# Attention's query transposes: whole words, two heads at a time, with the split into halves moved behind the transpose

## The chip, the cores and the metric

The kernel runs on one core of one Trainium2 chip. The metric is device time in microseconds (us), the median of several runs; lower is better. A core has TensorE (PE, matrix products and transposes, writing to PSUM), VectorE (DVE), ScalarE (ACT), GpSimd (POOL) and SyncE (SP), which issues the loads. In the profile, PEld is TensorE's loading of weights.

## The reference

One layer of a hybrid decoder block, for one sequence of 512 tokens and width 1024, float32 throughout. The input is normalised and projected once; two token mixers work side by side; their outputs are gated per channel, merged and projected again.

```python
h = rms_norm(x, norm_pre); proj = h @ w_in      # then split by columns
q_n = apply_rotary(q_n.reshape(B, S, 8, 64), nsa_ang)   # k_c, k_s, k_w too
o_a = nsa_sequence(q_n, k_c, v_c, k_s, v_s, k_w, v_w, gate)   # sparse attention
y_a = (o_a * silu(z_n)) @ w_nsa_o
o_b = retention_sequence(q_r, k_r, v_r)
y_b = (o_b * silu(z_r)) @ w_ret_o
x = x + rms_norm((sigmoid(m_a) * y_a + sigmoid(m_b) * y_b) @ w_out, norm_post)
```

The attention has 8 heads of 64 channels in two key groups, and three branches (compressed, selected, sliding window). Each head's scores are `q · k * 64 ** -0.5`, masked, put through softmax, and multiplied with the values. With 512 tokens there are only 8 selectable blocks, so every valid block is selected, and selected and sliding branch both see all earlier tokens.

## The kernel before

**Number format.** TensorE is fed in fp32r, the rounded form of float32. A float32 operand is split into a high half, rounded to fp32r, and a low half, the rest; three products (high-high, low-high, high-low) replace one. A split is a rounding copy (on ScalarE through `act`, or for weights on ScalarE or VectorE through `cp_any`) and a subtraction on VectorE (`sub_split`). The weights come as a stream of 128x1024 pieces into `raw`; `splitter` and `split_lo` turn each into two pieces `whi` and `wlo` of 512 columns, held in rings of nine.

**Order.** Every part is a Python generator, and `Order.run` chooses which goes on next by priority and by running estimates of when each engine is free (`Order.eng`, `Order.now`). What comes out is one fixed order of instructions per engine; at run time the engines wait for each other through semaphores. The choice of engine in `cp_any`, and of the engine for the softmax scaling in `att_head`, also goes by these estimates. Buffers that are passed around are in rings: four `NAT` tiles, two PSUM banks each for `ACC` (projections), `PS` (scores), `PT` (transposes) and `PO` (attention outputs).

**Stages.** `main` runs the large products in order: the keys and values of two branches, then 280 columns with the third, then the queries (four tiles of 128 tokens, t = 3, 2, 1, 0, all 512 columns of 8 heads), then `hidden` (the compression network, twice, with products of 256 columns), and then the gates, retention and output blocks. As each query tile's product ends, `tail_q(t)` takes it: a scaled copy from PSUM to a `NAT` tile (`qn`), the rotation (`rope16`), the split into halves, transposes, and a copy into `qT[t]`. When `qT[t]` and the keys are ready, `attention` starts `att_cmp` and the `att_head`s of that tile, whose blocks share TensorE with `main`.

**Layout of the queries.** `qT[t]` is 128 partitions by 8 heads by 128 tokens, fp32r. For each head the 64 channels' high half lies on partitions 0 to 63 and the low half on 64 to 127. The keys `kA` (high) and `kB` (low) hold the same 64 channels twice, on both halves of the partitions, so that one product sums over both halves of the query. The compressed keys `kc` are doubled in the same way. Before the transpose, the same memory (`qs`) holds the split halves in token order.

**Names in the profile.** The helpers have one line each: `act` is L189, `V.tensor_copy` in `cp_any` L197, `tt` (and so `sub_split`) L201, `ts` L210, `mm` L222, `tr` L226, the masked row maximum of `att_head` L801. `arena_r` holds all fp32r arrays (`qT`, keys, values), `arena_f` the float32 ones, `nat` the `NAT` tiles, `bank` all of PSUM. `ident` is the float32 identity for transposes and `identr` the same in fp32r; only `tail_q` uses `identr`.

Of the kernel before, what the change touches and what calls it, by code (L numbers as in the profile page):

```python
# [11 lines left out]
FR = mybir.dt.float32r  # L12
# [6 lines left out]
P = 128  # L19
# [12 lines left out]
LAG, PE_LAG = 55.0, 60.0  # L32
# [104 lines left out]
def block_kernel(ctx: ExitStack, tc, x, xT, x0s, ws, small, w2s, norm_post, rope_r, dmask, out):  # L137
# [10 lines left out]
    ep = ctx.enter_context(tc.tile_pool(name="end", bufs=1))  # L148
# [6 lines left out]
    def at(kb, n, dt=FT):  # L155
        o = int(kb * 256)
        return (arena_r if dt == FR else arena_f)[:, o:o + n]

    def f(ap):
        return ap.bitcast(FT)  # L160

    banks = [pp.tile([P, 512], FT, name=f"bank{i}") for i in range(8)]
    ACC, PS, PT, PO = (Ring(b, PE_LAG) for b in (banks[0:2], banks[2:4], banks[4:6], banks[6:8]))
# [15 lines left out]
    def act_ns(o, i, k=0):  # L179
        return 0.833 * size(o) + (51 if far(i) else 93) + 93 * k  # L180
# [4 lines left out]
    def lazy(*vals):  # L185
        return sum(v is not None and not isinstance(v, (int, float)) for v in vals)

    def act(o, i, func=AF.Copy, r=0.0, **kw):
        S.activation(o, i, func, **kw)  # L189
        return od.op("act", act_ns(o, i, lazy(kw.get("bias"), kw.get("scale"))) + (95 if "accum_out" in kw else 0), r)  # L190
# [9 lines left out]
    def tt(o, a, b, op, r=0.0, e="dve"):  # L200
        (V if e == "dve" else G).tensor_tensor(o, a, b, op=op)  # L201
        if op == OP.pow:
            return od.op(e, 300 + 164 * size(o), r, True)
        return od.op(e, (1.042 * size(o) + 69) if e == "dve" else (2.36 * size(o) + 77), r, e == "pool" or near(o, a, b))
# [20 lines left out]
    def tr(ps, a, idn, r=0.0):  # L225
        T.transpose(ps, a, idn)  # L226
        return od.pe(86 if a.dtype == FR else 108, r, 45.0 if a.dtype == FR else 31.0)
# [6 lines left out]
    def sub_split(lo, src, hi, r, e="dve"):  # L234
        return tt(lo, src, f(hi), OP.subtract, r, e)
# [4 lines left out]
    ident = cp.tile([P, P], FT, name="ident")  # L240
    make_identity(nc, ident)
    identr = cp.tile([P, P], FR, name="identr")
# [10 lines left out]
    qT = [at(4 * t, 1024, FR).rearrange("p (h c) -> p h c", h=8) for t in range(NT)]  # L253
# [228 lines left out]
    def rs(t, i=0):  # L482
        return rs3[:, i, t:t + 1]
# [16 lines left out]
    def rope16(v, t, shape, r, e="dve"):  # L500

        n = int(np.prod(shape))
        pat = {1: "p (a c) -> p a c", 2: "p (a b c) -> p a b c"}[len(shape)]
        kw = dict(zip("ab", shape))
        t1, t2 = (at(41 + 0.5 * i, n * 16).rearrange(pat, **kw) for i in range(2))

        def bc(a):
            c = a.shape[-1]
            for _ in shape:
                a = a.unsqueeze(1)  # L510
            return a.broadcast_to([P, *shape, c])
        ix = (slice(None),) * (1 + len(shape))
        lo, hi, al = ix + (slice(0, 8),), ix + (slice(8, 16),), ix + (slice(0, 16),)
        tt(t1, v[al], bc(ropen[:, t, 0:16]), OP.mult, r, e)
        tt(t2[lo], v[hi], bc(ropen[:, t, 16:24]), OP.mult, r, e)
        r = tt(t2[hi], v[lo], bc(ropen[:, t, 24:32]), OP.mult, r, e)
        return tt(v[al], t1, t2, OP.add, r, e)
# [184 lines left out]
    def tail_q(t, ps, e):  # L702
        qn = yield from NAT.get()
        yield e, "act"
        e = act(qn, ps, r=e, scale=rs(t, 1))
        ACC.put(ps, e)
        yield e, "dve"
        e = rope16(qn.rearrange("p (h c) -> p h c", h=8), t, (8,), e)
        qs = qT[t].rearrange("p h (s c) -> p h s c", s=2)
        qv = qn.rearrange("p (h c) -> p h c", h=8)  # L710
        e = act(qs[:, :, 0, :], qv, r=e)
        yield e, "dve"
        e = sub_split(qs[:, :, 1, :], qv, qs[:, :, 0, :], e)
        NAT.put(qn, e)
        for g in range(2):
            pt = yield from PT.get()
            yield e + PE_LAG
            for j in range(4):
                ep = tr(pt.bitcast(FR)[:, j * P:(j + 1) * P],
                        qs[:, g * 4 + j].rearrange("p a b -> p (a b)"), identr, e)  # L720
            yield ep, "act"
            ep = act(qT[t][:, g * 4:g * 4 + 4, :], pt.rearrange("p (h c) -> p h c", h=4), r=ep)
            PT.put(pt, ep)
        qready[t] = ep
        od.flags.add(f"q{t}")

# [468 lines left out]
    def main():  # L1195
# [29 lines left out]
        for t in reversed(range(NT)):  # L1225
            ps, e = yield from nat(blk, t, 512, t == 0)
            od.spawn(tail_q(t, ps, e), 1)
# [161 lines left out]
```

## Time and profile before

| | |
|---|---|
| median of 3 runs | 530.89 us (529.78 to 530.95) |
| span of the profiled execution, first to last instruction | 527.0 us |
| the profiled execution's own whole time | not listed; its span stands 3.9 us under the median |
| TensorE busy | 518.6 us (98%) |
| VectorE busy | 376.9 us (72%) |
| ScalarE busy | 272.8 us (52%) |
| GpSimd busy | 12.6 us (2%) |
| mean granted TensorE clock | 0.999 |

The median of the runs is what is compared between kernels. The span holds what the profile shows; around it lies time that no row covers. Busy shares are means over the whole span and hide that stages have different limits. A matmul's row is longer than the step to the next matmul, because matmuls overlap, so TensorE's rows are best read by their starts. The chain that ended last says which engine's work, or which wait, set the time of each stretch.

### The profile page before, as it was taken

To read this page: it belongs to the slowest core of one execution; us is meant where nothing else is said; L and a number is where in the kernel's file an instruction comes from. 1 tells how busy PE (TensorE), PEld (TensorE's weight loads), DVE (VectorE), ACT (ScalarE), POOL (GpSimd) and SP (SyncE) were. 2 spreads that over 40 slices of the span, in tenths; PEclk is the share of its full clock that TensorE was granted. 3 is DMA by queue.
4 is the path that set the end of the run, shared out by engine and by line. 5 is a ranking of instruction groups with operands and counts; after the bars stand their busy time and mean duration, and the time that the engine had idled before them with its cause. 6 is when DMAs were issued, how large, how long until landed. Compare 5 with 4: busy or idle time off the path is not lost.

```text
span 527.0 us, 7380 instructions
## 1 busy us (share of the span) xinstructions
PE 518.6 (98%) x2634; PEld 437.5 (83%) x2634; DVE 376.9 (72%) x921; ACT 272.8 (52%) x592; POOL 12.6 (2%) x32
## 2 busy tenths in 40 slices
PE   9999999999999999999999999999999999999995
PEld 7888788888888888888888888888888888888885
DVE  6699799889879999887886576777637335345533
ACT  6664698687657888574535253625304324123411
POOL 1000000000000000000000000000000000000000
PEclk9999999999999999999999999999999999999999
DMA  8951027502204004133131341131905134304032
GB/s 320 370 183 41 21 81 214 186 2 90 71 1 137 24 5 156 40 106 114 41 120 44 137 157 44 48 115 40 326 34 159 33 127 138 104 1 159 1 99 100
DMA packets 18133, 55.19 MB, mean 105 GB/s; under 512 B 1969, under 2 KB 3249, under 8 KB 18097
## 3 DMA queue, kind: packets, MB, share of 16 engines
q1 hardware_dynamic: 17952, 54.60, 31.0%
q8 instruction: 20, 0.33, 0.3%
q14 instruction: 17, 0.13, 0.1%
q10 hardware_dynamic: 144, 0.14, 0.1%
HBM read 52.63 MB, written 2.10 MB: 104 GB/s over the span
## 4 chain that ended last, share of the span: by engine, by line
PE 89%; DVE 4%; DMA 4%; issue 2%; ACT 1%; SPq 0%; POOLq 0%; DVEq 0%; POOL 0%
PE bank L222 82%; PE bank L226 6%; DMA raw<-in_stream_dram 4%; DVE wlo L201 1%; DVE arena_r L201 0%; DVE arena_f L801 0%; ACT arena_f L189 0%; DVE arena_f L210 0%; DVE whi L197 0%; DVE arena_f L201 0%; SPq L435 0%; DVE arena_f L214 0%; SPq L315 0%; DVE stat L218 0%; ACT whi L189 0%
## 5 line engine op out<-in xcount | busy, mean ns | idle before, releaser
L189 ACT ACTIVATE whi<-raw 128x512 fp32r<-128x512 f32 x148 | 88.5, 626 | 50.7 <-PE bank L222 43.6
L201 DVE TENSOR_TENSOR wlo<-raw,whi 128x512 fp32r<-128x512 f32 x160 | 103.6, 684 | 5.7 <-ACT whi L189 4.2
L222 PE MATMUL bank<-whi,hTh 128*128 128x512 f32 x256 | 100.4, 408 | 0.2 <-ACT hTh L189 0.2
L222 PE MATMUL bank<-whi,hTl 128*128 128x512 f32 x256 | 96.5, 392 | 0.0
L222 PE MATMUL bank<-wlo,hTh 128*128 128x512 f32 x256 | 96.1, 391 | 0.0
L222 PE MATMUL bank<-arena_r 128*128 128x256 f32 (+2 forms) x328 | 69.9, 335 | 0.0
L222 PE MATMUL bank<-hTh,whi 128*128 128x512 f32 x160 | 63.8, 399 | 0.0
L222 PE MATMUL bank<-hTh,wlo 128*128 128x512 f32 x160 | 62.5, 390 | 0.0
L222 PE MATMUL bank<-hTl,whi 128*128 128x512 f32 x160 | 62.4, 390 | 0.0
L189 ACT ACTIVATE arena_f<-arena_f,stat 128x512 f32<-128x512 f32 (+3 forms) x106 | 56.8, 560 | 6.2 <-DVE stat L218 2.8
L222 PE MATMUL bank<-arena_r,whi 128*128 128x512 f32 x192 | 59.1, 389 | 0.0
L189 ACT ACTIVATE arena_r<-bank 128x512 fp32r<-128x512 f32 (+2 forms) x80 | 44.6, 569 | 25.8 <-PE bank L226 25.5
L201 DVE TENSOR_TENSOR arena_r<-bank,arena_r 128x512 fp32r<-128x512 f32 (+2 forms) x72 | 46.6, 655 | 15.0 <-ACT arena_r L189 14.5
L222 PEld LDWEIGHTS bank<-whi,hTl 128*128 128x128 f32 x256 | 48.4, 189 | 10.8
L222 PEld LDWEIGHTS bank<-arena_r 128*128 128x128 f32 x328 | 51.6, 189 | 6.9 <-DVE arena_r L201 0.4
L222 PEld LDWEIGHTS bank<-whi,hTh 128*128 128x128 f32 x256 | 48.5, 190 | 8.8 <-ACT hTh L189 0.5
L222 PEld LDWEIGHTS bank<-wlo,hTh 128*128 128x128 f32 x256 | 48.3, 189 | 8.2
L222 PE MATMUL bank<-whi,arena_r 128*128 128x512 f32 (+1 forms) x176 | 49.2, 353 | 0.0
L222 PEld LDWEIGHTS bank<-arena_r,whi 128*128 128x128 f32 x192 | 36.0, 188 | 7.6 <-DVE sg L214 0.2
L226 PE MATMUL bank<-ident,arena_f 128*128 128x128 f32 (+1 forms) x244 | 36.7, 273 | 1.0 <-DVE arena_f L522 1.0
L222 PE MATMUL bank<-arena_r,wlo 128*128 128x512 f32 x96 | 37.4, 389 | 0.0
L222 PEld LDWEIGHTS bank<-whi,arena_r 128*128 128x128 f32 x176 | 32.1, 189 | 4.5
(125 smaller groups left out, 656.2 us busy)
## 6 DMA issues: line engine op xcount, KB each, us to landing
raw<-in_stream_dram SPq DMA_DIRECT2D x79, 512.0 KB, 4.1
arena_f<-in_x_dram SPq DMA_DIRECT2D x8, 512.0 KB, 7.0
arena_f<-in_rope_r_dram SPq DMA_DIRECT2D x8, 256.0 KB, 2.7
arena_f<-in_xT_dram SPq DMA_DIRECT2D x7, 256.0 KB, 5.9
out_dram<-arena_f SPq DMA_DIRECT2D x6, 256.0 KB, 2.1
raw<-in_stream_dram SPq DMA_DIRECT2D x4, 280.0 KB, 7.5
raw<-in_stream_dram SPq DMA_DIRECT2D x2, 256.0 KB, 3.2
arena_f<-in_norm_post_dram SPq DMA_DIRECT2D x1, 512.0 KB, 7.5
```

The source lines that it names most:

```text
L189: S.activation(o, i, func, **kw)
L201: (V if e == "dve" else G).tensor_tensor(o, a, b, op=op)
L222: T.matmul(ps, a, b, start=start, stop=stop)
L226: T.transpose(ps, a, idn)
```

## The change

Before, `tail_q` split the rotated queries in SBUF, transposed the halves as fp32r in two groups of four heads (each transpose takes the 128 columns of one head, high beside low), and copied each group from PSUM into `qT`. Now it transposes the rotated float32 queries, four transposes of 128 columns that each hold two heads. An even head then lies on partitions 0 to 63 of the PSUM bank and an odd head on 64 to 127. ScalarE rounds each half of the partitions into `qT` on the same partitions (the high halves), and VectorE subtracts these from the bank and writes the low halves to the other 64 partitions. So an even head has its high half on partitions 0 to 63, as before, and an odd head has the low half there. The keys are untouched, since they are the same on both halves. The `NAT` tile is given back after the transposes and no longer after the split; one `PT` bank is taken where two were, and it is given back after the last subtraction. Nothing outside `tail_q` differs in the source.

```diff
         e = rope16(qn.rearrange("p (h c) -> p h c", h=8), t, (8,), e)
-        qs = qT[t].rearrange("p h (s c) -> p h s c", s=2)
-        qv = qn.rearrange("p (h c) -> p h c", h=8)
-        e = act(qs[:, :, 0, :], qv, r=e)
-        yield e, "dve"
-        e = sub_split(qs[:, :, 1, :], qv, qs[:, :, 0, :], e)
+        pt = yield from PT.get()
+        yield e + PE_LAG
+        for i in range(4):
+            e = tr(pt[:, i * P:(i + 1) * P], qn[:, i * P:(i + 1) * P], ident, e)
         NAT.put(qn, e)
-        for g in range(2):
-            pt = yield from PT.get()
-            yield e + PE_LAG
-            for j in range(4):
-                ep = tr(pt.bitcast(FR)[:, j * P:(j + 1) * P],
-                        qs[:, g * 4 + j].rearrange("p a b -> p (a b)"), identr, e)
-            yield ep, "act"
-            ep = act(qT[t][:, g * 4:g * 4 + 4, :], pt.rearrange("p (h c) -> p h c", h=4), r=ep)
-            PT.put(pt, ep)
+        qp = qT[t].rearrange("p (i o) c -> p i o c", o=2)
+        pv = pt.rearrange("p (i c) -> p i c", i=4)
+        rows = (slice(0, 64), slice(64, P))
+        yield e, "act"
+        for o in range(2):
+            eh = act(qp[rows[o], :, o, :], pv[rows[o]], r=e)
+        yield eh, "dve"
+        for o in range(2):
+            ep = sub_split(qp[rows[1 - o], :, o, :], pv[rows[o]], qp[rows[o], :, o, :], eh)
+        PT.put(pt, ep)
         qready[t] = ep
```

## The prediction

> **What bounds the kernel now.** I read the page's busy shares first, then the chain that ended last, then the chain, the windows and the instruction timeline of the stretch in which the queries are handled.
>
> ```profile
> span 527.0 us, 7380 instructions
> PE 518.6 (98%) x2634; PEld 437.5 (83%) x2634; DVE 376.9 (72%) x921; ACT 272.8 (52%) x592; POOL 12.6 (2%) x32
> PE 89%; DVE 4%; DMA 4%; issue 2%; ACT 1%; SPq 0%; POOLq 0%; DVEq 0%; POOL 0%
> ```
>
> The span is 3.9 us under the median of the runs, 530.89; the sum below is made against the span, and its difference is carried to that median. TensorE (PE) carries 89% of the chain, so removing TensorE time pays almost everywhere. The exception matters here: the chain leaves TensorE just where the queries are prepared.
>
> ```profile
> 61.99 0.60 ACT arena_r L189
> 77.14 0.61 DVE wlo L201
> 77.80 1.22 PE bank L222 x7
> 57.10:61.70 4.60, 4.60 (x30) 3.57 (x29) 2.58 (x9) 2.84 (x6) 0.00 (x0) 1.00 0.00 0
> 61.70:73.15 11.45, 11.45 (x59) 9.53 (x58) 10.48 (x39) 10.70 (x26) 0.00 (x0) 1.00 0.16 48
> 73.15:77.80 4.65, 4.51 (x33) 3.78 (x31) 4.58 (x12) 4.44 (x9) 0.00 (x0) 1.00 0.15 38
> ```
>
> The first three rows are of the chain (start, length, engine, tile, line): from 61.99 to 77.75 us it runs (its first and last piece stand here) through ScalarE (ACT) and VectorE (DVE), and it returns to TensorE at 77.80, behind a low half of a weight (wlo). The last three are windows (stretch, length, then busy us of PE, PEld, DVE, ACT, POOL, then the granted clock, 1.00, and DMA). VectorE is idle for 2.02 of the first 4.60 us, then for 0.97 of 11.45 and 0.07 of 4.65. TensorE looks full, but a matmul row contains its neighbours' overlap. By starts:
>
> ```profile
> 73.66 0.35 PE L222 MATMUL bank<-whi,arena_r 128*128 128x256 f32 x1
> 73.96 0.28 PE L222 MATMUL bank<-whi,arena_r 128*128 128x256 f32 x1
> 74.08 0.28 PE L222 MATMUL bank<-wlo,arena_r 128*128 128x256 f32 x1
> 77.30 0.36 PE L222 MATMUL bank<-whi,arena_r 128*128 128x256 f32 x1
> 77.80 0.38 PE L222 MATMUL bank<-wlo,arena_r 128*128 128x256 f32 x1
> 79.01 0.54 PE L226 MATMUL bank<-identr,arena_r 128*128 128x128 f32 x4
> ```
>
> A 256-column matmul starts 0.12 after the last (73.96 to 74.08), but 0.50 passes at 77.30. From 73.66 to 79.01 (5.35 us) there stand 24 such matmuls (2.83), two of 512 columns (0.45), two groups of four full-word transposes (0.88, priced below) and 0.08 for a change of kind: 4.24. So TensorE loses about 1.1 us there, all to weights that VectorE finishes late.
>
> **The change, part by part.** It touches `tail_q`, run four times (t = 3, 2, 1, 0).
>
> *TensorE.* Eight fp32r transposes per tile, in two groups of four, become one group of four in f32.
>
> ```profile
> 58.12 0.39 PE L222 MATMUL bank<-whi,hTl 128*128 128x512 f32 x1
> 58.35 0.46 PE L226 MATMUL bank<-identr,arena_r 128*128 128x128 f32 x4
> 58.65 0.46 PE L222 MATMUL bank<-whi,hTh 128*128 128x512 f32 x1
> 58.95 0.40 PE L222 MATMUL bank<-wlo,hTh 128*128 128x512 f32 x1
> 362.62 0.40 PE L222 MATMUL bank<-hTh,wlo 128*128 128x512 f32 x1
> 362.86 0.60 PE L226 MATMUL bank<-ident,arena_f 128*128 128x128 f32 x4
> 363.21 0.47 PE L222 MATMUL bank<-hTh,whi 128*128 128x512 f32 x1
> 363.53 0.39 PE L222 MATMUL bank<-hTl,whi 128*128 128x512 f32 x1
> ```
>
> The fp32r group takes 0.30 from its start to the next matmul's, and that matmul 0.30 where the usual step is 0.23 (58.12 to 58.35): 0.37 in all. The f32 group takes 0.35, and the matmul behind it 0.32: 0.44. Per tile 2 x 0.37 - 0.44 = 0.30 goes, 1.2 us in four tiles. Where they lie:
>
> ```profile
> 71.91 0.46 PE L226 MATMUL bank<-identr,arena_r 128*128 128x128 f32 x4
> 73.36 0.46 PE L226 MATMUL bank<-identr,arena_r 128*128 128x128 f32 x4
> 80.97 0.45 PE L226 MATMUL bank<-identr,arena_r 128*128 128x128 f32 x4
> ```
>
> Tile 1's two groups fall where the chain is on VectorE; their 0.3 pays only if VectorE moves too. The other tiles' groups, from 58.35 on and at 79.01 and 80.97, stand on TensorE's part of the chain. So 0.9 to 1.2.
>
> [...]
>
> *ScalarE.* Per tile it did a rounding copy from SBUF (arena_r<-nat) and two copies out of PSUM; it now does two rounding copies out of PSUM, on 64 partitions each but still 512 elements long.
>
> ```profile
> 59.11 0.63 ACT L189 ACTIVATE arena_r<-nat 128x512 fp32r<-128x512 f32 x1 [1.31 <-DVE nat L201]
> 59.65 1.07 ACT L189 ACTIVATE arena_r<-bank 128x512 fp32r<-128x512 f32 x2
> L189 ACT ACTIVATE nat<-bank 64x512 f32<-64x512 f32 x8 | 4.7, 593 | 3.4 <-PE bank L222 3.3
> L189 ACT ACTIVATE arena_r<-bank 128x512 fp32r<-128x512 f32 x64 | 37.3, 591 | 18.6 <-PE bank L226 18.3
> ```
>
> Half the partitions cost the same (593 against 591 ns; that 64-partition row also writes other partitions than it reads). In a row such a copy takes 0.54, so one is saved per tile: 2.2 us in all.
>
> *VectorE.* One subtraction of 128x512 from SBUF becomes two of 64x512 from PSUM, written to the other 64 partitions.
>
> ```profile
> L201 DVE TENSOR_TENSOR nat<-bank,nat 64x512 f32<-64x512 f32 x8 | 5.5, 686 | 2.4 <-ACT nat L189 2.4
> 75.86 0.68 DVE L201 TENSOR_TENSOR arena_r<-bank,arena_r 128x512 fp32r<-128x512 f32 x1
> 76.47 0.68 DVE L201 TENSOR_TENSOR arena_r<-nat,arena_r 128x512 fp32r<-128x512 f32 x1
> ```
>
> 686 against 680 ns: again no discount for half the partitions, and a step of 0.61. So 0.6 us is *added* per tile, 2.4 in all, on the engine that bounds the stretch. No row of VectorE writes 64 partitions across; the ends for it are 0.55 (the nearest shorter operation, a 512-column scaling) and twice 0.61, and I take 0.61, since ScalarE's row above crosses at no cost. [...]
>
> Where do the 2.4 us go? Tiles 3 and 2 fall before 61.70, into 2.0 us of idle time, and cost nothing. Tiles 1 and 0 put 1.2 into a full VectorE. Against it stands ScalarE's relief: the program chooses the engine of weight roundings (`cp_any`) and of the softmax scaling by which is free sooner, and in the full stretch VectorE did these:
>
> ```profile
> L210 DVE TENSOR_SCALAR arena_f<-arena_f,stat,gate 128x512 f32<-128x512 f32 x3 | 1.6, 546 | 0.1
> L197 DVE CAST whi<-raw 128x512 fp32r<-128x512 f32 x2 | 0.8, 420 | 0.0
> ```
>
> Tiles 2, 1 and 0 free about 1.6 us of ScalarE in it, room for two or three of these five, each 0.34 to 0.55 of VectorE: 0.7 to 1.5 back, about the 1.2 added. I take VectorE's balance as zero, and TensorE's 1.1 us of waiting as unchanged; the ends are both rivals.
>
> *Waits and buffers.* The subtraction now waits for ScalarE's copies, which wait for TensorE's transposes; before, only for a copy. Behind it in VectorE's queue stand weight halves and attention heads. The one transposing bank is held through transposes, two copies and two subtractions, 0.4 + 1.1 + 1.2 = 2.7 us, where two were held 0.3 + 0.5 each; attention blocks draw on the same two banks. I cost it at nothing, because TensorE has projection matmuls between (58.65 and on); without that cover it is the 0.9 us longer per tile. No DMA is issued, moved or passed; POOL and SP are untouched.
>
> **Sum.** -0.9 to -1.2 from TensorE, 0 from VectorE: -1.1, so a span of 525.9, and 529.8 for the median.
>
> **Rivals.**
>
> 1. *Attention starts earlier and the wait goes too.* The way from rotated query to first score is shorter.
>
> ```profile
> 55.76 0.29 DVE L201 TENSOR_TENSOR nat<-arena_f 128x128 f32<-128x128 f32 x1
> 57.42 0.68 DVE L201 TENSOR_TENSOR arena_r<-nat,arena_r 128x512 fp32r<-128x512 f32 x1
> 60.96 0.70 PE L222 MATMUL bank<-arena_r 128*128 128x512 f32 x2
> 61.70 0.69 DVE L801 CUSTOM_DVE_ANT_0 arena_f<-bank,maskp 128x512 f32<-128x512 f32 x1 [1.23 <-PE bank L222]
> ```
>
> Now 4.9 us pass from the rotation's end (56.05) to the first score matmul (60.96). With 0.4 of transposes, 1.1 of copies, 1.2 of subtractions and about 1 of hand-overs (my estimate) it is 3.7, so the heads' work starts some 1.2 us earlier, in VectorE's idle time, and the 1.1 us lost at 73.66 to 79.01 goes. -1.2 - 1.1 = -2.3: 528.6. Against it: the projections of tiles 2 to 0 compete for ScalarE, and the order may spend the head start on heads and not on weight halves.
>
> 2. *VectorE's queue stalls (slower).* If VectorE reaches each first subtraction before ScalarE's copies are done, it stands idle with weight halves queued behind. Its wait for a copy was 0.76 here at tile 2:
>
> ```profile
> 59.78 0.69 DVE L201 TENSOR_TENSOR arena_r<-nat,arena_r 128x512 fp32r<-128x512 f32 x1 [0.76 <-ACT arena_r L189]
> ```
>
> For tiles 2, 1 and 0: 3 x (0.6 + 0.76) = 4.1, less TensorE's 0.9: +3.2, 534.1. It decides from 2.5 us of uncovered VectorE time (TensorE's 0.9 and the 1.6 of a change that can be told); below that the kernel is not slower. Against it: the stretch's other work is ready and interleaved.
>
> [...]
>
> 4. *The order shifts elsewhere.* The program writes its whole instruction order from its own running estimate, so a changed tail can move work as far as 330 us. The price is one missed hand-over, up to the 0.5 seen at 77.30, in either direction; it widens the range.
>
> **How the numbers follow.** Forecast 0.46, its own range 529.0 to 530.7; earlier start 0.35; stall 0.16; four passes 0.01; 0.02 for what I don't see, on the slow side. "Same" is within 0.3%, 1.6 us, about what a measurement of this kernel can tell from no change: 529.3 to 532.5. The forecast's lower edge gives 0.06 to faster, the earlier start 0.33 (0.02 of it stops above 529.3), so faster 0.39; of the stall and the rest, 0.15 pass 532.5; same 0.46. The range for eight in ten runs from 527.6 (the earlier start with two hand-overs gained) to 532.9 (the stall with half of each wait: 3 x (0.6 + 0.38) - 0.9 = +2.0).
>
> **What would show it.** In the changed kernel's trace: 16 more f32 transposes and none in fp32r; 8 subtractions of 64x512 at about 686 ns; 4 fewer ScalarE copies; first score matmul near 59.8; more weight roundings and scalings on ScalarE between 60 and 80. Right, if TensorE's starts between 73 and 79 still lose about 1 us; earlier start, if they lose under 0.3; stall, if VectorE's idle time before the new subtractions exceeds 2 us and weight halves come late behind them. The prediction is wrong if f32 groups take well over 0.44, if the crossing subtraction takes over 0.7, or if waits appear past 84 us, where TensorE is full now.

## The result, and the profile after

The kernel got slower: median 535.57 us (532.77 to 536.67, 6 runs) against 530.88 (529.78 to 531.22), a ratio of 1.0097, 95% interval 1.0074 to 1.012. The forecast was 529.8.

Runs of one and the same version differ by up to 5 us, the longer ones with a lower mean granted TensorE clock, so besides medians the text gives the runs at a mean clock of 0.997 or more, "at full clock". Of the changed kernel's six runs only the profiled one, 532.77 at 0.999, is such; the others had 0.990 to 0.993. So two things are to be explained: 4.0 us of span at full clock (531.0 against 527.0), and why most runs lost more.

The page after, in the same places as before:

```profile
span 531.0 us, 7360 instructions
PE 518.2 (98%) x2618; PEld 435.8 (82%) x2618; DVE 379.6 (71%) x926; ACT 272.3 (51%) x589; POOL 12.9 (2%) x32
PE 84%; DVE 7%; DMA 4%; issue 2%; ACT 2%; SPq 0%; POOLq 0%; DVEq 0%; POOL 0%; ACTq 0%
```

TensorE has 16 instructions less and VectorE 2.7 us more, near what the edit says. What moved is the chain: TensorE carries 84% of it where it had 89%. The waits of TensorE (line, releaser, total, times, longest) show for what; first the kernel before, all of its rows:

```profile
PE bank L1277 <- DVE rsrow L239: 1.0, 1, 1.0
PE bank L226 <- DVE arena_f L522: 1.0, 1, 1.0
PE bank L222 <- ACT hTh L189: 0.2, 1, 0.2
```

and the rows that the changed kernel has beside these:

```profile
PE bank L222 <- DVE arena_r L214: 2.6, 2, 1.9
PE bank L226 <- DVE arena_r L201: 1.3, 3, 0.5
PE bank L222 <- DVE wlo L201: 0.4, 1, 0.4
```

That is 4.3 us of new waits; with 1.2 us of transposes saved, +3.1 of the +4.0. The other 0.9 is in small steps (a row counts only the idle time, and the first matmuls after a wait also start slower: 2.33 us pass between the starts around the longest wait, of which 1.94 is idle and 0.23 the usual step); it is not assigned further.

**The 1.3 us: the transposing banks.** Two groups of transposes for attention blocks (at 73.01 and 83.56) wait for the query subtractions, and tile 0's query transposes (78.19) for an attention block's. TensorE's timeline around the last:

```profile
82.76 0.28 PE L222 MATMUL bank<-wlo,arena_r 128*128 128x256 f32 x1
83.56 0.66 PE L226 MATMUL bank<-ident,arena_f 128*128 128x128 f32 x4 [0.52 <-DVE arena_r L201]
```

and the chain there (start, length):

```profile
82.11 0.69 DVE arena_r L201
82.81 0.69 DVE arena_r L201
```

The chain's two rows are tile 0's two subtractions of 64x512. The attention block's transposes need the bank that these read; it comes free at 83.50 and TensorE goes on at 83.56, 0.8 us after the matmul ahead, where the usual step is 0.12. The old tail gave its banks back after a copy.

**The 2.6 us: an accumulator bank, 150 us later.** TensorE, ScalarE and VectorE around 239 us:

```profile
238.68 0.39 PE L222 MATMUL bank<-whi,hTl 128*128 128x512 f32 x1
241.01 0.50 PE L222 MATMUL bank<-whi,hTh 128*128 128x512 f32 x1 [1.94 <-DVE arena_r L214]
239.11 0.69 ACT L189 ACTIVATE arena_r<-bank,rs 128x512 fp32r<-128x512 f32 x1 [1.86 <-PE bank L222]
236.49 1.88 DVE L201 TENSOR_TENSOR wlo<-raw,whi 128x512 fp32r<-128x512 f32 x3
238.89 0.86 DVE L214 SCALAR_TENSOR_TENSOR nat<-bank,rs,arena_f 128x256 f32<-128x256 f32 x2
240.21 0.75 DVE L214 SCALAR_TENSOR_TENSOR arena_r<-bank,rs,arena_r 128x512 fp32r<-128x512 f32 x1
240.87 0.87 DVE L214 SCALAR_TENSOR_TENSOR nat<-bank,rs,arena_f 128x256 f32<-128x256 f32 x2
```

Retention's first value block ends on TensorE with the matmul at 238.68, and ScalarE and VectorE empty its bank at 239.11 and 240.21; only then does the second value block start. All blocks of `main` take the two `ACC` banks in turn, except here. In the order that the program wrote out, the banks of `main`'s blocks (84 and 85 are the numbers of the two) from the 20th on, counted from 0:

```
before: ... 20 bank_84, 21 bank_85, 22 bank_84, 23 bank_85, ...
after:  ... 20 bank_84, 21 bank_85, 22 bank_84, 23 bank_84, ...
```

Block 21's bank is still held, because its tail (`tail_qk`, tile 3) reads it with the four operations at 238.89 and 240.87, behind the weight halves at 236.49 in VectorE's queue. Had block 23 taken that bank, it would have had to wait until 241.74. In the kernel before, the tail's last two reads come earlier, and TensorE does not wait:

```profile
238.10 0.87 DVE L214 SCALAR_TENSOR_TENSOR nat<-bank,rs,arena_f 128x256 f32<-128x256 f32 x2
```

So what is late is the tail in VectorE's queue; that the same bank was given twice follows from it. Nothing of the edit is near: the program's running estimate chose another order.

### The profile page after: what moved, and what is told of

It is laid out like the page before. It is cut to its first block, busy times and chain, and to the rows that moved or that the text cites. A ratio compares the mean times of both kernels' runs of the same rounds, so it can differ in the third digit from the quotient of the medians.

```text
span 531.0 us, 7360 instructions
## 1 busy us (share of the span) xinstructions
PE 518.2 (98%) x2618; PEld 435.8 (82%) x2618; DVE 379.6 (71%) x926; ACT 272.3 (51%) x589; POOL 12.9 (2%) x32
## 4 chain that ended last, share of the span: by engine, by line
PE 84%; DVE 7%; DMA 4%; issue 2%; ACT 2%; SPq 0%; POOLq 0%; DVEq 0%; POOL 0%; ACTq 0%
PE bank L222 78%; PE bank L226 6%; DMA raw<-in_stream_dram 4%; DVE wlo L201 3%; DVE arena_r L201 2%; ACT arena_f L189 1%; DVE arena_f L801 1%; DVE arena_f L201 0%; ACT arena_r L189 0%; DVE arena_f L210 0%; DVE whi L197 0%; DVE arena_r L214 0%; SPq L435 0%; ACT whi L189 0%; DVE arena_f L214 0%
## 5 line engine op out<-in xcount | busy, mean ns | idle before, releaser
L189 ACT ACTIVATE arena_r<-bank 128x512 fp32r<-128x512 f32 (+3 forms) x80 | 45.4, 570 | 41.9 <-PE bank L226 41.3
L201 DVE TENSOR_TENSOR arena_r<-bank,arena_r 128x512 fp32r<-128x512 f32 (+3 forms) x80 | 52.2, 660 | 19.3 <-ACT arena_r L189 18.5
L226 PEld LDWEIGHTS bank<-ident,arena_f 128*128 128x128 f32 (+1 forms) x244 | 29.2, 138 | 9.5 <-DVE arena_r L201 1.8
```

## The experiments

Theory A is that the loss lies in the order written anew, theory B that it is VectorE's doubled subtraction. Each run stood beside runs of the kernel before on the same chip; their medians were 529.25 to 529.69.

**The new tail in the old order.** The tail issues four transposes, two copies and two subtractions at the place where the old one copied its first group, and tells the estimate the old tail's costs:

```diff
-        e = act(qs[:, :, 0, :], qv, r=e)
...
+        e = od.op("act", act_ns(qs[:, :, 0, :], qv), e)
...
+            if g == 0:
+                for o in range(2):
+                    S.activation(qp[rows[o], :, o, :], pv[rows[o]], AF.Copy)
+                for o in range(2):
+                    V.tensor_tensor(qp[rows[1 - o], :, o, :], pv[rows[o]], f(qp[rows[o], :, o, :]), op=OP.subtract)
```

(An `od.op` line counts a cost and issues nothing; `...` stands for lines left out.)

> The new transposes, copies and subtractions, but the running estimate in the order is fed the costs and steps of the old query tail, so that every other instruction stands on its engine where it stood before the change. Theory A (the loss comes from the order written anew: the 2.1 us wait near 239 us, the 0.9 us near 270 us, and the lower clock behind them): those waits are gone, TensorE's 1.2 us are saved, and VectorE's extra 2.4 us cost at most 1.2: 529.5 to 531.0 us, clock 0.999 in all runs. Theory B (the loss is VectorE's doubled subtraction itself, in a stretch that VectorE bounds): still at least 533 us.

Measured: 539.54 us (537.72 to 540.73), ratio 1.0181 [1.0154, 1.0208]. By its number this meets theory B's condition (533 or more), but not its cause. Past 95 us TensorE has no wait, as A said; the loss is all in the query stage (and in an early wait, 2.1 us where it was 1.0, that differs from run to run). VectorE's timeline:

```profile
62.44 1.39 DVE L731 TENSOR_TENSOR arena_r<-bank,arena_r 64x512 fp32r<-64x512 f32 x2 [2.13 <-ACT arena_r L729]
65.88 1.39 DVE L731 TENSOR_TENSOR arena_r<-bank,arena_r 64x512 fp32r<-64x512 f32 x2 [2.04 <-ACT arena_r L729]
```

VectorE stands idle before each of the four pairs, 2.13, 2.04, 2.69 and 1.06 us, with heads and weight halves behind it: 7.9 us, where its added work is some 3. This is the stall of the second rival in pure form, and it says that the new tail needs an order of its own: the old one is worse for it than the one the program wrote. So it does not part A from B, except that the late waits go with the order.

**One subtraction left out, the order kept.** The estimate counts both, one is issued (GpSimd's writing of the zeros is not shown).

```diff
-            ep = sub_split(qp[rows[1 - o], :, o, :], pv[rows[o]], qp[rows[o], :, o, :], eh)
+            if o:
+                ep = od.op("dve", 1.042 * 512 + 69, eh, False)
+            else:
+                ep = sub_split(qp[rows[1 - o], :, o, :], pv[rows[o]], qp[rows[o], :, o, :], eh)
```

> The changed kernel with its order kept, but the odd heads' subtraction is not issued (their low halves are left at zero, written once by GpSimd while it is idle), so VectorE does 2.4 us less. Theory B: the waits of TensorE between 60 and 100 us, 1.3 us above before, go, and the waits further on with them: 531 us or less. Theory A: the 1.3 us go at most, the waits near 239 and 270 us stay: 533 to 535 us.

Measured: 533.2 us (532.74 to 534.85); the one run at full clock is 532.74, beside the changed kernel's 532.77. Waits:

```profile
PE bank L222 <- DVE arena_r L214: 2.6, 2, 1.9
PE bank L226 <- DVE arena_r L201: 0.6, 1, 0.6
PE bank L222 <- DVE wlo L201: 0.7, 1, 0.7
```

With four subtractions less for VectorE the bank wait of the query stage halves (1.3 to 0.6): the two waits for the query subtractions are gone, and the wait of tile 0's transposes for an attention block's bank stays. The weights' wait is 0.7 for 0.4, but the second trace of the changed kernel (the next run) has 0.7 as well, so the 0.3 more is not shown to come of the missing subtraction. The 2.6 us stay to the digit. They belong to the order. B falls as the main cause, and the expectation of A, that the 1.3 us go at most and the late waits stay, holds; the median came at its lower edge. Beside its own runs of the kernel before it stands 3.9 us behind by medians, the changed kernel 4.7; the intervals of the ratios overlap.

**The changed kernel once more, for its clock.**

> The changed kernel once more, for a trace of an execution with the lower mean clock (0.990 to 0.993 in five of its six runs, 0.999 in the profiled one). If the clock falls because TensorE stood idle for 2 us near 239 us, the windows behind that place show a granted clock well under 1.0 for a few us, and the span is 533 to 535; if the lower clock has another cause, it lies elsewhere.

Measured: 533.89 us, clock 0.993. Its windows around the wait (columns as before; the third figure from the right is the granted clock):

```profile
238.09:241.50 3.41, 1.48 (x7) 0.92 (x6) 3.34 (x11) 1.97 (x5) 0.00 (x0) 1.00 0.71 253
241.50:244.90 3.40, 3.40 (x14) 2.90 (x13) 1.10 (x3) 1.42 (x3) 0.00 (x0) 0.50 0.27 77
```

and the second stretch in the profiled run at 0.999:

```profile
241.50:244.90 3.40, 3.40 (x21) 2.86 (x20) 2.01 (x5) 1.50 (x3) 0.00 (x0) 1.00 0.29 90
```

Behind the wait the clock is granted at half for 3.4 us: 14 instructions of TensorE are done where 21 were. This execution is 0.43 us ahead of the profiled one where the wait ends (240.58 against 241.01) and 1.14 behind where the next one ends (272.37 against 271.23), so the half clock cost 1.6 us. The span, 532.1, is 1.1 over the profiled 531.0, under the 533 to 535 expected; the place of the half clock is as expected. Of a run at 0.990 (spans of 534.3 to 534.9) there is no trace; what lowered its clock further stays open.

**The same loss without the change.** One constant of the running estimate is changed in the kernel before, and then also in the changed one.

```diff
-LAG, PE_LAG = 55.0, 60.0
+LAG, PE_LAG = 56.0, 60.0
```

> The kernel before, with one constant of the order's running estimate changed from 55 to 56 ns; the query tail is the old one. In the order that comes out, one projection block (the 23rd) is given the same accumulator bank as the block ahead of it, as in the changed kernel; in the kernel before no block is. Theory A (the loss lies in the order): a wait of 2 us near 238 us as in the changed kernel, 532.5 to 535, although nothing of the change is in it. Theory B (the loss is the doubled subtraction): 530 to 531.

> The changed kernel with the same constant, 56: no block is given the bank of the block ahead of it. Theory A: no wait over 1 us past 200 us, the clock 0.999 in most runs, 530 to 532. Theory B: 533 or more.

Measured: the kernel before with 56, 534.89 us (534.04 to 535.04), ratio 1.0097 [1.008, 1.0113]; the changed kernel with 56, 530.79 (529.45 to 534.58), ratio 1.0033 [1.0012, 1.0053], with three of ten runs at 0.999, where most were expected. The old kernel's waits show a pair of the same size at 241.69 and 273.50 us, the changed kernel's have none on L214:

```profile
PE bank L222 <- DVE nat L214: 1.9, 1, 1.9
PE bank L222 <- DVE arena_r L214: 0.7, 1, 0.7
```

The expectation that a block here takes the bank of the block ahead of it is not borne out. The rows around the wait:

```profile
240.77 0.87 DVE L214 SCALAR_TENSOR_TENSOR nat<-bank,rs,arena_f 128x256 f32<-128x256 f32 x2
241.56 0.74 DVE L214 SCALAR_TENSOR_TENSOR arena_r<-bank,rs,arena_r 128x512 fp32r<-128x512 f32 x1
241.69 0.50 PE L222 MATMUL bank<-whi,hTh 128*128 128x512 f32 x1 [1.88 <-DVE nat L214]
```

The second value block starts at 241.69, while the first one's bank is read until 242.30. So it has the other bank, and waited for the last reads of `tail_qk`, which end at 241.64. The late tail costs 1.9 us with the banks in turn as well.

So a change of one unit (a nanosecond) in the estimate costs the old kernel a loss of the size that the edit cost, and takes most of it from the new one. Not all of the old kernel's loss is the pair: TensorE also waits 2.1 us between 75 and 95 us there, where the kernel before waits for nothing. This settles A for the large part.

**How far an order alone moves the time.** Three more settings of constants: the first two each in both kernels, the third in the changed one.

```diff
-MARGIN = 50.0
+MARGIN = 60.0
...
-LAG, PE_LAG = 55.0, 60.0
+LAG, PE_LAG = 54.0, 60.0
...
-SLACK = 700.0
+SLACK = 900.0
```

> The kernel before with another constant of the order (MARGIN) at 60 for 50: another order, no block with the bank of the block ahead of it. Both theories: within 1.5 us of the kernel before, and how far it is tells how much an order alone moves the time.

> The changed kernel with MARGIN at 60, no block with the bank of the block ahead of it. Theory A: within 1 us of the run before it in this list (1.2 us less of transposes, up to 1.3 us more of waits between 60 and 100 us), 530 to 532. Theory B: 2 us or more above it.

> The kernel before with the constant at 54, its partner. If the kernel before owes its time to one good order, this one is slower than it by 1 us or more, and the changed kernel with the same constant is no slower than this; if the change itself costs, it is about as fast as the kernel before and the changed kernel behind it.

> The changed kernel with the constant 55 at 54, another order without such a block: 529 to 532 by theory A; 533 or more by theory B.

> The changed kernel with SLACK at 900 for 700, another order without a block on the bank of the block ahead of it: 529 to 532 by theory A; 533 or more by theory B.

Medians in us, and in brackets those of the runs at full clock, with their number:

| constant | kernel before | changed kernel |
|---|---|---|
| 55, as given | 529.25 to 530.88 by series (529.1, 10 of 24 of one) | 535.57 (532.77, 1) |
| 56 | 534.89 (534.04, 1) | 530.79 (530.38, 5) |
| 54 | 529.24 (528.84, 7) | 530.33 (529.78, 5) |
| MARGIN 60 | 532.72 (none) | 531.30 (530.64, 5) |
| SLACK 900 | not run | 535.15 (none) |

The old kernel spans 5.6 us over four orders, the changed one 5.2 over five: the sign of the difference depends on the constant. Both expectations for MARGIN 60 were missed: the old kernel stands 3.3 us above the kernel before beside it, though none of its four runs was at full clock, and the changed one 1.4 us below the old, where 1 was expected at most. The query stage depends on the order too: between 70 and 97 us TensorE waits 2.1 us in the old kernel with 56 and with MARGIN 60 and for nothing with 55 and 54; in the changed kernel it waits 1.7 to 2.1 us with the other constants, and 2.7 with SLACK 900. And 54 does not bear out that the old kernel owes its time to one lucky order: there it is as fast (ratio 1.0 [0.9981, 1.0018]) with another order. In the cleanest pair, 54, the changed kernel stands 0.9 us behind at full clock, with two waits that its partner lacks, the same as in the changed kernel: 1.3 us for the transposing banks and 0.4 for a weight. 1.3 + 0.4 - 1.2 = +0.5 of the 0.9. SLACK 900 missed A's range though no block doubles its bank. Its waits lie in the query stage, where a load came late and VectorE stood, then both subtractions held the transposing bank. VectorE's rows and TensorE's:

```profile
83.86 0.43 DVE L197 CAST whi<-raw 128x512 fp32r<-128x512 f32 x1 [0.88 <-DMA raw<-in_stream_dram]
84.31 1.39 DVE L201 TENSOR_TENSOR arena_r<-bank,arena_r 64x512 fp32r<-64x512 f32 x2
85.76 1.12 PE L226 MATMUL bank<-ident,arena_f 128*128 128x128 f32 x4 [1.63 <-DVE arena_r L201]
```

and the window behind:

```profile
85.60:88.90 3.30, 3.14 (x11) 2.75 (x12) 3.13 (x9) 2.67 (x5) 0.00 (x0) 0.50 0.35 108
```

So there is a second way to the same loss, and the edit has a part in it: the bank held longer, and half clock behind the wait. The late load, 0.88 us of VectorE's time, has the other; why it came late is not shown.

**One step of the order mended.** In the changed kernel, the tail whose bank was late is not held back for VectorE's backlog:

```diff
-        yield max(e, rtr[0]), "dve"
+        yield max(e, rtr[0]) if (hp, t) == (0, 3) else (max(e, rtr[0]), "dve")
```

> The changed kernel, with one step of the order altered: the tail of one block (retention's queries and keys, first pair of heads, last tile) is no longer held back until VectorE's backlog is small. Up to there all engines have the order of the changed kernel; from there the two accumulator banks alternate. Theory A: the 2.1 us wait near 239 us and the 0.9 us near 270 us go, and with them the half-clock window behind: 529.5 to 531.0. If the waits stay or only move, the reading of the bank is wrong: 533 or more.

Measured: 532.25 us (530.76 to 534.59), ratio 1.0056 [1.0034, 1.0077]; at full clock 530.76 and 531.56. Half as expected: the wait near 270 us is gone, and there is no half clock behind 243 us, but a wait remains there, and the median missed A's range:

```profile
243.84 0.50 PE L222 MATMUL bank<-whi,hTh 128*128 128x512 f32 x1 [0.88 <-DVE nat L214]
```

The tail's last two reads of its bank still come behind five weight halves in VectorE's queue. So the root is VectorE's backlog at that place, as with 56 above. The step moved the tail and let the banks alternate at once, so it does not tell what each is worth.

**One subtraction left out in a clean order.**

> The changed kernel with the constant at 54 (the run e10, an order without long waits past 100 us), its order kept, but the odd heads' subtraction is not issued (their low halves are zero, written once by GpSimd), so VectorE does 2.4 us less. If the doubled subtraction costs the local 1.3 us of TensorE's waits between 60 and 100 us, TensorE's waits there fall by 0.8 us or more against e10 and the undisturbed time by as much, to 528.5 to 529.0; if the waits there hang on the order and the chain of copies alone, it stays at 529.3 to 530.0.

Measured: 529.3 us (528.35 to 531.3), ratio 0.9994 [0.998, 1.0008]; at full clock 529.39 (5 runs) against 529.78 with both. Two rows of waits in the query stage are the same as in the run above without the second subtraction: 0.6 us for the transposing banks where it was 1.3, and 0.7 for a weight where it was 0.4.

It stays in the range of the second answer, 0.4 us lower than with both, and the bank and weight waits together fall by 0.4, not by 0.8. But the two were run on different chips. Beside the runs of the kernel before on its own chip, this one is level at full clock (0.05 us over 529.34) and 0.4 ahead by medians, where the one with both subtractions was 0.7 and 1.1 behind: a gain of 0.6 or 1.5. The bound of 0.997 is rough, too: the traced run, 528.74 us at 0.996, has half clock only after its last matmul. The intervals of the two kernels against the one before overlap (1.0015 [0.9995, 1.0036] for both subtractions). So the second subtraction may cost from some tenths of a microsecond to 1.5 here, and which of the two answers holds is open. No version here beat the kernel before by more than its interval.

## Why the prediction was wrong, step by step

**The step that failed** is rival 4: "The order shifts elsewhere ... The price is one missed hand-over, up to the 0.5 seen at 77.30". The mechanism was named and the size was wrong. An accumulator bank's hand-over behind VectorE's backlog measured 1.9 us, with a second of 0.7, and in three of the four traces with such a wait half clock stood behind it, 1.6 us in the run traced for it, which the prediction did not have at all. With it failed a term of the sum, the waits and buffers put at nothing: the transposing banks cost 1.3 us and a late weight 0.4. Less the 1.2 of the transposes this is 3.1 of the 4.0 us at full clock; 0.9 stays open. A price taken from the worst wait in a good order is no bound for another order. The test that was stated, waits past 84 us, is what came.

**Transposes: right.** The f32 group behind tile 3's rotation, on TensorE:

```profile
56.50 0.60 PE L226 MATMUL bank<-ident,nat 128*128 128x128 f32 x4
56.86 0.48 PE L222 MATMUL bank<-whi,hTh 128*128 128x512 f32 x1
57.17 0.40 PE L222 MATMUL bank<-wlo,hTh 128*128 128x512 f32 x1
```

0.36, and 0.31 for the next step: 0.44 as forecast, 16 of them. No run shows the price in four passes to which the forecast gave 0.01: the f32 group costs 0.44, and a group of four fp32r transposes cost 0.37.

**Copies and subtractions: prices right, the step a little low.**

```profile
L189 ACT ACTIVATE arena_r<-bank 64x512 fp32r<-64x512 f32 x8 | 4.7, 588 | 0.7 <-PE bank L226 0.7
L201 DVE TENSOR_TENSOR arena_r<-bank,arena_r 64x512 fp32r<-64x512 f32 x8 | 5.5, 689 | 0.8 <-ACT arena_r L189 0.6
```

588 and 689 ns, against 593 and 686 forecast; the rows show no price for crossing to the other 64 partitions. But the pair on the chain (82.11, 82.81, 83.50) takes 0.70 a piece, not the 0.61 of the steps before, so a tile adds 0.8 and not 0.6; whether the crossing makes the longer step is not shown. VectorE's idle time before the eight subtractions is 0.8 us in all, under the 2 us named for the stall.

**"I cost it at nothing": wrong.** The bank held for 2.7 us was to be covered by projection matmuls. It cost 1.3 us in the orders with 55, 56 and 54 alike, in three waits of 0.25 to 0.54, where 0.9 per tile was named for the case without cover. The projections did not cover, because they stand behind the waiting transposes in TensorE's order: the one behind those at 83.56 starts at 83.97.

**VectorE's balance of zero: the relief did not come.** The groups of VectorE between 61.7 and 78 us:

```profile
L210 DVE TENSOR_SCALAR arena_f<-arena_f,stat,gate 128x512 f32<-128x512 f32 x4 | 2.2, 546 | 0.1
L197 DVE CAST whi<-raw 128x512 fp32r<-128x512 f32 x1 | 0.4, 419 | 0.0
```

Four scalings and one rounding, where there were three and two: none of the relief by ScalarE came. With one subtraction of each tile gone, the bank wait fell by 0.7 us in two orders and the weight's wait rose by 0.3, a rise that the changed kernel's own second trace shows as well. So 0.4 to 0.7 us of waits, of the 4.7 by medians, is what VectorE's own added work explains in the traces; the times of the last run leave room for 1.5.

**The earlier start: half right.** VectorE and TensorE at the first scores:

```profile
59.62 1.14 PE L222 MATMUL bank<-arena_r 128*128 128x512 f32 x4
60.35 1.39 DVE L201 TENSOR_TENSOR arena_r<-bank,arena_r 64x512 fp32r<-64x512 f32 x2 [0.44 <-ACT arena_r L189]
61.77 0.69 DVE L801 CUSTOM_DVE_ANT_0 arena_f<-bank,maskp 128x512 f32<-128x512 f32 x1
```

The first score matmul came at 59.62, forecast 59.8; but the first row maximum at 61.77, where it was at 61.70. Tile 2's subtractions stood ahead of it and waited for ScalarE. The head start was spent in VectorE's queue, a small stall of the kind of the second rival. The 1.1 us that TensorE lost to late weights did go, as this rival said: from 75.23 to 77.38 its 256-column matmuls start 0.12 apart. The waits for the transposing banks took its place.

## What to carry to other kernels

A kernel whose order is written out by an estimate has to be compared over several orders, old and new alike: here one nanosecond in a constant moved the old version by 5.5 us and the new one by about 3 (each beside its own runs of the kernel before), more than the edit was to bring. Count how long an edit holds each shared bank and what stands in order behind whoever waits for it, and price a late hand-over by the backlog that can stand ahead of the last reader, not by the worst wait of the order at hand. And where VectorE bounds a stage, a subtraction on half the partitions is priced as a whole one: here 64x512 took 689 ns and 128x512 687.

## What the runs showed of the hardware

Behind several of the longer waits of TensorE stands a stretch at half clock, 3.4 us long in the run traced for it. That stood behind the waits of 1.88 to 1.94 us near 240 us in three of the four traces that have them, where 512-column matmuls start 0.42 to 0.43 us apart for 0.23 (not in the profiled run of the changed kernel), behind the 1.63 us wait above, and behind the 2.40 us wait at 82.36 of the new tail in the old order, where 256-column matmuls start 0.21 us apart at 85.20 and 0.12 at 83.30. The same trace has a wait of 1.82 us at 68.05, and behind it the 512-column matmuls keep their step of 0.23. An early wait for the doubled keys differs from trace to trace, from 0.4 to 3.5 us: half clock stood behind it where it was 1.92 us (the changed kernel with 56), 3.31 (with the one step mended) and 3.45, and not where it was 1.01 (the kernel before), 1.12 (the changed one), 1.20 (the changed one with 54) and 1.71 (the same with one subtraction left out). It was longest in the old kernel with 54:

```profile
33.59 0.66 PE L226 MATMUL bank<-ident,arena_f 128*128 128x128 f32 x2 [3.45 <-DVE arena_f L522]
```

and behind it the 280-column matmuls go at 0.23 us a step, up to 38.67, where they went at 0.13.

On what it hangs is not shown. The two traces of the changed kernel have the same wait of 1.94 us near 240 us, and half clock stood behind the one and not behind the other; in the run at 0.993 TensorE was busy for 1.48 of the 3.41 us ahead of the half clock (238.09 to 241.50, above). So the length of a wait alone does not tell whether it costs another 1.6 us behind it.
